# A five-stage network on one core: ScalarE and VectorE held to the order of emission, which is made with durations read from a trace

## The chip, the core and the metric

The kernel runs on one core of one Trainium2 chip. The core has a matrix engine (TensorE, PE in the profile; its weight loads are PEld), a vector engine (VectorE, DVE), a scalar engine (ScalarE, ACT), GpSimd (POOL), and SyncE (SP), which issues most of the DMAs. The metric is the device time of one execution in microseconds (us), the median of the runs.

## The reference

All data are fp32, one sequence of 1024 tokens (1040 with 16 meta tokens in the last two layers), 1024 features. Two blocks run one behind the other:

```python
def first_block(x, ...):
    f1 = swiglu(rms_norm(x, ffn1_pre_g), w_gate, w_up, w_down)      # D_FF 2816
    x = x + 0.5 * rms_norm(f1, ffn1_post_g)
    m = token_mixer(rms_norm(x, mix_pre_g), w_in, ...)              # 8 forget-gate + 4 differential heads
    x = x + rms_norm(m, mix_post_g)
    f2 = swiglu(rms_norm(x, ffn2_pre_g), ...)
    return x + 0.5 * rms_norm(f2, ffn2_post_g)

def second_block(x, meta, ...):
    h = jnp.concatenate([meta_b, x], axis=1)
    h = rglru_ssd_layer(h, ...)        # "even": conv, gated linear scan, chunked state-space scan
    h = stick_breaking_layer(h, ...)   # "odd": 16 heads of 64
    return rmsnorm(h, final_norm)[:, N_META:]

def stick_breaking_block(q_blk, k_ctx, v_ctx, q0):
    z = q_blk @ k_ctx.T * SB_HEAD_DIM ** -0.5
    log_keep = jnp.where(before, log_sigmoid(-z), 0.0)
    csum = jnp.cumsum(log_keep, axis=-1)
    weights = jnp.where(before, jnp.exp(log_sigmoid(z) + csum[..., -1:] - csum), 0.0)
    return weights @ v_ctx
```

## The kernel before

**Stages.** By the trace the first feed-forward stage runs to some 685 us, the mixer (attention of 8 + 4 heads) to some 1305, the second feed-forward stage to some 1980, the even stage to some 2740 and the odd stage (attention with 16 heads) to the end. Activations lie feature by token in SBUF as a pair `Ah`, `Al`: a value rounded to fp32r and what is left over. Each matrix product is three matmuls (`mm3`, L336 to L338: hi x hi, lo x hi, hi x lo). So every operand of TensorE comes from two instructions, one behind the other: ScalarE copies the hi half, VectorE subtracts it for the lo half. Weights (`wh`, `wl`), the transposed probabilities of attention (`th`, `tl`, written from the PSUM tile `ptr`), values (`v`, from `pv`) and activations all go through that pair.

**Attention.** `psc` are scores, ScalarE turns them into `kt` and `pt`, TensorE transposes `pt` into `ptr` (L1607), ScalarE and VectorE make `th` and `tl` of it, and TensorE multiplies them with the values into `po` (L1587). In the odd stage VectorE runs a running product over `kt` (`tensor_tensor_scan`, L2275) and a product into `pt` (L2279) for each piece of scores, ahead of the transposes. `pv` is the projection of the values of one token tile, through two PSUM buffers that VectorE frees when it has written `v`.

**Even stage.** `pe` are the projections, `xb` their copy; VectorE runs four-tap convolutions over it (`xc`, `cv`; 128x1040), products with gates (`sz`, L2601, which frees the `pe` buffer; `t`, L2609), the linear scan (`t`, L3015), and the state-space work of a chunk (`S`, `ea`, `xd`, `dec`, `et`, `ab`, `cbm`). `psx`, `psb`, `pso`, `psy`, `pst` are PSUM tiles of the latter.

**Two orders.** Work is written as generator threads. `Sched` (L109) steps the thread that can start earliest by a model of durations, with priorities; each thread yields ("A", us), ("V", us), ("P", us) ahead of an instruction of ScalarE, VectorE or TensorE, and the model's functions `act(n)`, `dve(n)` and `pool_tt(n)` give the us for n elements of a row. That sets the order in which instructions are emitted. When the program is complete, the framework's own list scheduler sets the order of each engine's queue from the dependencies, with durations of its own; in this kernel it may move instructions of every engine past each other. In the queues of before, 1141 of VectorE's 5036 instructions and 560 of ScalarE's 3228 (table loads not counted) stand behind one with a later number of emission; on TensorE it is 467 of 19667. An engine runs its queue in order. A table of ScalarE's functions is loaded where the queue needs another one (58 loads); `act_set`, `act_need` and `after_pin` tie some functions to a load.

Of the kernel before, what the change touches and what calls it, by code (L numbers as in the profile page):

```python
# [18 lines left out]
P = 128  # L19
# [3 lines left out]
L = M + S  # L23
# [73 lines left out]
def act(n):  # L97
    return 0.07 + 0.92e-3 * n


def dve(n, speed=1):
    return 0.08 + 1.045e-3 * n / speed


def pool_tt(n):
    return 0.2 + 2.1e-3 * n

# [93 lines left out]
class Ctx:  # L201
    def __init__(self, ctx, tc):
# [9 lines left out]
        self.ahead = None  # L212
        self.dr = ctx.enter_context(tc.tile_pool(name="dr", bufs=1, space=DRAM))
        self.ident = self.const.tile([P, P], F32, name="ident")
        make_identity(nc, self.ident)
# [5 lines left out]
        self.last = None  # L221
        for nm in ("activation", "copy"):
            def f(*a, _o=getattr(nc.scalar, nm), **k):
                self.last = _o(*a, **k)  # L224
                return self.last
            setattr(nc.scalar, nm, f)
        self.onesm = self.const.tile([P, P], F32, name="onesm")
        nc.vector.memset(self.onesm, 1.0)

    def new_A(self):  # L230
        return (self.ap.tile([P, KD, L], F32R, tag="Ah", name="Ah"),
                self.ap.tile([P, KD, L], F32R, tag="Al", name="Al"))

    def after_pin(self, ins):
# [6 lines left out]
    def act_set(self, name):  # L241

        ins = self.after_pin(self.nc.scalar.preload_act_table_set(name))
        if self.last is not None and self.last is not self.pin:
            self.tc.add_manual_dep(ins.ins, self.last.ins.name, mybir.DependencyInfo(
                mybir.DependencyClass.NoSync, mybir.DependencyReason.DATA), reason="table set")
        self.pin = ins

# [334 lines left out]
class Rows:  # L583
# [15 lines left out]
    def put(self, t, y, junk):  # L599
# [3 lines left out]
        if g not in self.ss:  # L603
            self.ss[g] = c.small.tile([P, len(ms)], F32, tag=f"ss{len(ms)}", name="ss", bufs=5)
        if self.dram is not None:
            r0 = self.row0 + t * P
            c.nc.scalar.dma_start(self.dram[r0:r0 + P, :], y)
        tt = yield ("A", act(1024))
        c.nc.scalar.activation(junk(), y, AF.Square, accum_out=self.ss[g][:, t - g:t - g + 1])
        self.stored[t].set(tt + 3.0)  # L610
# [1163 lines left out]
def mixer_stage(c, A, rows0, prm, w_in, forget_b, lams, subln, rope, w_out, gpost, res, rows):  # L1774
# [3 lines left out]
    with ExitStack() as ctx:  # L1778
# [18 lines left out]
        def gate_evac(lf, tok, ps):  # L1797
# [17 lines left out]
            if tok is HALVES[1]:  # L1815
                cum = pm.tile([8, S], F32, tag="bc", name="cum", bufs=2)
                yield ("V", dve(1024))
                nc.vector.tensor_tensor_scan(cum, c.one[:8].to_broadcast([8, S]), lf, 0.0, op0=ALU.mult, op1=ALU.add)
# [137 lines left out]
        def softmax(segs, m, pt, cb, ev, r):  # L1956
# [3 lines left out]
            for s, ps in enumerate(segs):  # L1960
                yield ("V", dve(m))
                if cb is not None:
# [7 lines left out]
            for s, ps in enumerate(segs):  # L1970
                t = yield ("A", act(m))
                nc.scalar.activation(pt[:, s * m:s * m + m], ps[:, :m], AF.Exp, bias=mx[:, 0:1], scale=-1.0,
                                     accum_out=sm[:, s:s + 1])
                T.r_ps["sc"].release(t)
            yield ("V", 0.2 * ns)
            if ns == 2:
# [213 lines left out]
def odd_stage(c, A, rows0, prm, w_in, w_out, res, final, out):  # L2190
# [3 lines left out]
    with ExitStack() as ctx:  # L2194
# [68 lines left out]
        def weights(ps, w, kt, k0, m, before, scanned, done):  # L2263
# [8 lines left out]

            t = yield ("V", dve(m))
            rev = kt[:, k0:k0 + m][:, ::-1]
# [224 lines left out]
def even_stage(c, A, rows0, prm, w_in, lru_wa, lru_wx, dt_bias, a_log, ssd_d, w_out, meta, res, rows, later):  # L2499
# [168 lines left out]
    def dt_rest():  # L2668
# [21 lines left out]
        nc.vector.tensor_scalar(l, dt, na, None, op0=ALU.mult)  # L2690
        yield ("V", dve(L))
        nc.vector.tensor_tensor_scan(ac, cut, l, 0.0, op0=ALU.mult, op1=ALU.add)
# [287 lines left out]
    def lru_rest(b, h, r, ig, t_, v):  # L2980
# [31 lines left out]
        for j in range(2):  # L3012
            u = 2 * b + j
            t = yield ("V", dve(LH, 0.5))
            nc.vector.tensor_tensor_scan(t_[:, j], r[:, j], v[:, j], 0.0 if h == 0 else carry[:, u:u + 1], op0=ALU.mult,  # L3015
# [293 lines left out]
```

## Time and profile before

| | us |
|---|---|
| median of 3 runs | 3579.32 |
| lowest, highest | 3578.43, 3579.59 |
| the profiled execution: own time | 3577.13 |
| its span, first to last instruction | 3575.4 |
| TensorE busy in it | 3430.7 |
| VectorE busy | 2749.9 |
| ScalarE busy | 1700.6 |
| GpSimd busy | 326.1 |

The profiled execution is 2.2 us below the median. Times in the rows below are us from the start of the span. A wait is listed by the engine that waited, the tile it wrote, and the instruction whose end released it.

### The profile page before, as it was taken

How to read it: one execution, taken by the hardware profiler on the slowest of the kernel's cores; microseconds unless marked ns; L12 is line 12 of the kernel's file. 1: busy time of each engine (PE TensorE's matmuls, PEld its weight loads, DVE VectorE, ACT ScalarE, POOL GpSimd, SP SyncE). 2: the span in 40 equal slices, each digit the busy share in tenths (PEclk: the TensorE clock that was granted, in tenths of full speed). 3: DMA queues.
4: the chain of work that ended last, by engine and by line, in shares of the span. 5: the costliest groups of instructions: out<-in, count | busy, mean ns of one | idle time of the engine just before them, and what ended most of it. 6: DMA issues, size and time to landing. Idle time of an engine off the chain costs nothing.

```text
span 3575.4 us, 51885 instructions
## 1 busy us (share of the span) xinstructions
PE 3430.7 (96%) x19675; PEld 2925.6 (82%) x19675; DVE 2749.9 (77%) x5050; ACT 1700.6 (48%) x3451; POOL 326.1 (9%) x355
## 2 busy tenths in 40 slices
PE   8999999899999999999999899998999999999998
PEld 6788888678888877888888899988878888888877
DVE  8876699988888769666799779578633688878784
ACT  5323245556666643232345447447422465656561
POOL 0111144000000001111351000000000000000000
PEclk9999999999999999999999999999999999999999
DMA  5542372311211551323552334244473110111133
GB/s 183 178 132 89 113 284 83 128 58 44 73 41 36 179 168 60 123 89 109 195 197 72 108 64 86 61 87 90 139 244 95 57 36 28 33 31 31 33 134 107
DMA packets 305842, 366.07 MB, mean 102 GB/s; under 512 B 18644, under 2 KB 221568, under 8 KB 305592
## 3 DMA queue, kind: packets, MB, share of 16 engines
q1 hardware_dynamic: 299800, 341.71, 30.7%
q10 hardware_dynamic: 5792, 21.04, 1.6%
q8 instruction: 155, 2.54, 0.3%
q14 instruction: 95, 0.78, 0.1%
HBM read 267.58 MB, written 95.13 MB: 101 GB/s over the span
## 4 chain that ended last, share of the span: by engine, by line
PE 73%; DVE 17%; ACT 4%; issue 3%; DMA 2%; SPq 0%; POOL 0%; DVEq 0%; ACTq 0%; POOLq 0%
PE pst L337 7%; PE pst L336 7%; PE pst L338 7%; PE po L1587 3%; PE pe L336 3%; PE pe L338 3%; PE pe L337 3%; DVE kt L2275 3%; PE pdn L337 2%; PE pdn L338 2%; PE pdn L336 2%; PE ptr L1607 2%; PE pwo L3100 2%; PE pwo L3101 2%; PE pwo L3102 2%
## 5 line engine op out<-in xcount | busy, mean ns | idle before, releaser
L336 PE MATMUL pe<-Ah,wh 128*128 128x260 f32 (+1 forms) x1184 | 340.6, 288 | 21.9 <-DVE sz L2601 8.2
L338 PE MATMUL pe<-Ah,wl 128*128 128x260 f32 (+1 forms) x1184 | 337.1, 285 | 0.0
L337 PE MATMUL pe<-Al,wh 128*128 128x260 f32 (+1 forms) x1184 | 336.4, 285 | 0.0
L224 ACT CAST wh<-w 128x512 fp32r<-128x512 f32 x280 | 162.1, 619 | 252.7 <-PE pst L337 160.2
L942 DVE TENSOR_TENSOR sg<-sg,pst 128x512 f32<-128x512 f32 x280 | 187.1, 684 | 104.8 <-PE pst L338 104.4
L1006 POOL TENSOR_TENSOR h<-h 128x512 f32<-128x512 f32 x88 | 136.2, 1547 | 1332.9 <-DVE h L988 1327.7
L337 PE MATMUL pst<-Al,wh 128*128 128x512 f32 x640 | 253.7, 396 | 0.0
L336 PE MATMUL pst<-Ah,wh 128*128 128x512 f32 x640 | 252.2, 394 | 0.0
L338 PE MATMUL pst<-Ah,wl 128*128 128x512 f32 x640 | 252.1, 394 | 0.0
L473 DVE TENSOR_TENSOR wl<-w,wh 128x512 fp32r<-128x512 f32 x280 | 212.0, 784 | 50.4 <-ACT wh L224 49.0
L336 PEld LDWEIGHTS pe<-Ah,wh 128*128 128x128 f32 (+1 forms) x1184 | 223.4, 189 | 26.2 <-DVE sz L2601 8.5
L337 PE MATMUL pdn<-dl,dh 128*128 128x512 f32 x592 | 230.8, 390 | 1.9 <-DVE dl L1099 1.9
L224 ACT CAST th<-ptr 128x512 fp32r<-128x512 f32 (+2 forms) x344 | 171.6, 515 | 125.4 <-PE ptr L1607 78.7
L338 PE MATMUL pdn<-dh,dl 128*128 128x512 f32 x592 | 230.3, 389 | 0.0
L1552 DVE TENSOR_TENSOR tl<-ptr,th 128x512 fp32r<-128x512 f32 (+2 forms) x344 | 197.5, 592 | 41.8 <-ACT th L224 38.4
L336 PE MATMUL pdn<-dh 128*128 128x512 f32 x592 | 229.1, 389 | 0.0
L337 PEld LDWEIGHTS pe<-Al,wh 128*128 128x128 f32 (+1 forms) x1184 | 223.0, 189 | 1.0
L338 PEld LDWEIGHTS pe<-Ah,wl 128*128 128x128 f32 (+1 forms) x1184 | 222.8, 188 | 0.8
L2275 DVE TENSOR_TENSOR_SCAN kt<-kt,onec 128x392 f32<-128x392 f32 (+5 forms) x224 | 204.2, 916 | 16.8 <-ACT kt L224 14.9
L224 ACT CAST wh<-wr 128x1024 fp32r<-128x1024 f32 (+2 forms) x116 | 119.0, 1026 | 182.7 <-PE pwo L3101 80.3
L336 PE MATMUL pst<-T,wh 128*128 128x512 f32 x480 | 187.3, 393 | 8.7 <-ACT T L224 8.7
L337 PE MATMUL pst<-T,wh 128*128 128x512 f32 x480 | 188.1, 392 | 0.4 <-DVE T L835 0.4
(550 smaller groups left out, 10023.6 us busy)
## 6 DMA issues: line engine op xcount, KB each, us to landing
hD<-h SPq DMA_DIRECT2D x22, 1792.0 KB, 8.1
w<-in_ffn_w_gate_dram SPq DMA_DIRECT2D x20, 1024.0 KB, 5.4
w<-in_ffn_w_up_dram SPq DMA_DIRECT2D x20, 1024.0 KB, 8.0
d<-hD SPq DMA_DIRECT2D x18, 1024.0 KB, 5.4
wr<-in_even_w_in_dram SPq DMA_DIRECT2D x36, 512.0 KB, 4.3
wo<-prer SPq DMA_DIRECT2D x32, 512.0 KB, 3.6
wr<-in_odd_w_in_dram SPq DMA_DIRECT2D x32, 512.0 KB, 4.3
wr<-in_w_in_dram SPq DMA_DIRECT2D x24, 512.0 KB, 3.9
```

The lines of the kernel that those rows point to most:

```text
L224: self.last = _o(*a, **k)
L336: nc.tensor.matmul(ps, wh, xh, start=start, stop=False)
L337: nc.tensor.matmul(ps, wh, xl, start=False, stop=False)
L338: nc.tensor.matmul(ps, wl, xh, start=False, stop=stop)
L473: (nc.gpsimd if eng == "G" else nc.vector).tensor_sub(lo, raw, hi.bitcast(F32))
L942: nc.vector.tensor_add(dst, src, ps)
L1006: nc.gpsimd.tensor_sub(q[:, o], q[:, a], q[:, b_])
L1552: nc.vector.tensor_sub(tl[:rows, :n], ptr[:rows, :n], th[:rows, :n].bitcast(F32))
L1587: nc.tensor.matmul(po[:, 256 - n:256], vs, (th, tl)[w][:rows, o:o + n], start=(x == 0 and y == 0 and 0 in which), stop=(x == last and y == ...
L1607: nc.tensor.transpose(ptr[:rows, o:o + P], pts[i][:, col:col + rows], c.ident)
L2275: nc.vector.tensor_tensor_scan(rev, rev, c.one.to_broadcast([P, m]), kt[:, k0 + m:k0 + m + 1], op0=ALU.mult, op1=ALU.mult)
L3100: nc.tensor.matmul(ps[n], oh, wh[:, sl], start=(first and k == 0), stop=False)
```

## The change

- The functions of the model get other numbers: `act`, `dve` and `pool_tt`, a new `scan(n)` for the four `tensor_tensor_scan` places, 0.14 us more on a mask add with a reduction, 0.19 us more on an exponential that also sums.
- Every instruction of ScalarE and VectorE that goes through the wrapped methods is recorded, and gets a dependency without a semaphore on the one recorded before it on the same engine. The list scheduler can't pass them by each other any more. TensorE, SyncE and GpSimd stay free.
- In `Rows.put` the DMA that stores the rows, issued from ScalarE's queue, stands behind the Square activation and not ahead of it.

```diff
 def act(n):
-    return 0.07 + 0.92e-3 * n
+    return 0.16 + 0.87e-3 * n
 
 
 def dve(n, speed=1):
-    return 0.08 + 1.045e-3 * n / speed
+
+    return (0.15 if speed == 1 else 0.21) + 1.05e-3 * n / speed
+
+
+def scan(n):
+    return 0.22 + 2.08e-3 * n
+
+
+ACCUM = 0.19
 
 
 def pool_tt(n):
-    return 0.2 + 2.1e-3 * n
+    return 0.2 + 2.6e-3 * n
...
-        for nm in ("activation", "copy"):
-            def f(*a, _o=getattr(nc.scalar, nm), **k):
-                self.last = _o(*a, **k)
-                return self.last
-            setattr(nc.scalar, nm, f)
+        self.tail = {}
+        self.strict = True
+
+        def record(e, ins):
+            if e == "A":
+                self.last = ins
+            if e in self.tail:
+                self.behind(ins, self.tail[e])
+            if self.strict:
+                self.tail[e] = ins
+            return ins
+
+        self.record = record
+        for e, eng, names in (("A", nc.scalar, ("activation", "copy")), ("V", nc.vector, (
...
+                def f(*a, _o=getattr(eng, nm), _e=e, **k):
+                    was, self.inner = self.inner, True
+                    ins = _o(*a, **k)
+                    self.inner = was
+                    return ins if was else record(_e, ins)
+                setattr(eng, nm, f)
...
+    def behind(self, ins, first):
+
+        self.tc.add_manual_dep(ins.ins, first.ins.name, mybir.DependencyInfo(
+            mybir.DependencyClass.NoSync, mybir.DependencyReason.DATA), reason="order of emission")
...
-        self.pin = ins
+        self.pin = self.record("A", ins)
...
+        tt = yield ("A", act(1024))
+        c.nc.scalar.activation(junk(), y, AF.Square, accum_out=self.ss[g][:, t - g:t - g + 1])
         if self.dram is not None:
             r0 = self.row0 + t * P
-            c.nc.scalar.dma_start(self.dram[r0:r0 + P, :], y)
-        tt = yield ("A", act(1024))
-        c.nc.scalar.activation(junk(), y, AF.Square, accum_out=self.ss[g][:, t - g:t - g + 1])
+            c.behind(c.nc.scalar.dma_start(self.dram[r0:r0 + P, :], y), c.last)
...
-            t = yield ("V", dve(m))
+            t = yield ("V", scan(m))
             rev = kt[:, k0:k0 + m][:, ::-1]
             nc.vector.tensor_tensor_scan(rev, rev, c.one.to_broadcast([P, m]), kt[:, k0 + m:k0 + m + 1],
```

The number of instructions is the same, but for ScalarE's table loads: 54 in place of 58. The queues differ nearly everywhere: 359 of VectorE's 5036 instructions keep their place in it. The lists below call a scan SCALAR_TENSOR_TENSOR too. In the queues of the change 96 of VectorE's instructions and 4 of ScalarE's stand behind one with a later number of emission, and 546 of TensorE's. All recorded instructions carry L251, the line of the wrapper.

The first of two places is VectorE's queue in the odd stage, where two heads' scans and the values of one token tile meet. The rows of before (`v4`, `v5`: the values of two heads; `tl`: lo halves of transposed probabilities):

```order
L1552 TENSOR_TENSOR tl_30252<-ptr_30250,th_30251 128x512
L1505 TENSOR_TENSOR v4_29862<-pv_30201,v4_29862 128x128
L1552 TENSOR_TENSOR tl_30271<-ptr_30269,th_30270 128x384
L1505 TENSOR_TENSOR v5_29864<-pv_30201,v5_29864 128x128
L2275 SCALAR_TENSOR_TENSOR kt_30285<-kt_30285,onec_76 128x392
L2279 TENSOR_TENSOR pt_30284<-pt_30284,kt_30285 128x392
L2275 SCALAR_TENSOR_TENSOR kt_30285<-kt_30285,onec_76 128x392
L2279 TENSOR_TENSOR pt_30284<-pt_30284,kt_30285 128x392
L1632 TENSOR_TENSOR oo_30205<-po_30234,ot_30332 64x256
```

The same place with the change, VectorE again:

```order
L251 SCALAR_TENSOR_TENSOR kt_30395<-kt_30395,onec_76 128x352
L251 TENSOR_TENSOR pt_30394<-pt_30394,kt_30395 128x352
L251 SCALAR_TENSOR_TENSOR kt_30395<-kt_30395,onec_76 128x344
L251 TENSOR_TENSOR pt_30394<-pt_30394,kt_30395 128x344
L251 SCALAR_TENSOR_TENSOR kt_30395<-kt_30395,onec_76 128x344
L251 TENSOR_TENSOR pt_30394<-pt_30394,kt_30395 128x344
L251 SCALAR_TENSOR_TENSOR kt_30419<-kt_30419,onec_76 128x456
L251 TENSOR_TENSOR pt_30416<-pt_30416,kt_30419 128x456
L251 SCALAR_TENSOR_TENSOR kt_30419<-kt_30419,onec_76 128x456
L251 TENSOR_TENSOR pt_30416<-pt_30416,kt_30419 128x456
L251 TENSOR_TENSOR v5_29860<-pv_30223,v5_29860 128x128
L251 TENSOR_TENSOR v4_29858<-pv_30273,v4_29858 128x128
```

Before, a pair `v4`, `v5` of one `pv` stands between the `tl` and ahead of the scans of `kt`. Now the `v5` of `pv_30223` and both of `pv_30273` come behind five scans and their products.

The second place is VectorE's queue in the even stage, in the first pass over a chunk of the state-space work. Before, around the update of the state `S`:

```order
L473 TENSOR_TENSOR wl<-wr,wh 128x1024
L2609 TENSOR_TENSOR t<-t,sz 128x260
L2770 TENSOR_SCALAR ab<-ab,dT 128x128 x4
L2826 TENSOR_TENSOR S_18696<-S_18696,et 128x512
L2835 TENSOR_TENSOR ea<-ea,pso 128x512
L3002 TENSOR_TENSOR v<-v,t 128x1040
L2601 TENSOR_TENSOR sz<-sz,pe 128x260
L2828 TENSOR_TENSOR S_18696<-S_18696,pst 128x512
L2838 TENSOR_TENSOR ea<-ea,psy 128x512
L2749 TENSOR_TENSOR cbm<-psb,mask_tri 128x128
```

The same place with the change, from the last of `xc` to the gate product `sz` that frees the projection's buffer:

```order
L251 SCALAR_TENSOR_TENSOR xc_18371<-xc_18371,dcol,ea 128x128
L251 SCALAR_TENSOR_TENSOR xc_18490<-xc_18490,dcol,ea 128x128
L251 TENSOR_TENSOR cbm<-psb,mask_tri 128x128
L251 SCALAR_TENSOR_TENSOR t<-r,carry,v 128x520
L251 TENSOR_TENSOR xd<-psx,dT 128x512
L251 TENSOR_TENSOR dec<-ab,dT 128x8
L251 COPY et<-ab 128x8
L251 TENSOR_SCALAR ab<-ab,dT 128x128 x8
L251 CAST lh<-cv_19271 128x520
L251 TENSOR_TENSOR ll<-cv_19271,lh 128x520
L251 TENSOR_TENSOR t<-t,sz 128x260
L251 TENSOR_TENSOR sz<-sz,pe 128x260
```

Before, `sz` comes two places behind the `ea` that reads `pso`. Now it stands behind both updates of `S`, both of `ea`, the four `xc`, `cbm`, a scan, `xd` and the eight `ab` of the next chunk.

## Rows read from the trace of the kernel before

**Rows 1.** The page: span; busy us of each engine (share, instructions)

```profile
span 3575.4 us, 51885 instructions
...
PE 3430.7 (96%) x19675; PEld 2925.6 (82%) x19675; DVE 2749.9 (77%) x5050; ACT 1700.6 (48%) x3451; POOL 326.1 (9%) x355
```

**Rows 2.** The page: the chain that ended last, share by engine

```profile
PE 73%; DVE 17%; ACT 4%; issue 3%; DMA 2%; SPq 0%; POOL 0%; DVEq 0%; ACTq 0%; POOLq 0%
```

**Rows 3.** Waits of TensorE, whole span: us, times, longest us

```profile
PE po L1587 <- DVE tl L1552: 22.2, 31, 2.8
PE po L1587 <- ACT th L224: 10.6, 13, 1.5
...
PE pst L336 <- ACT T L224: 8.7, 4, 4.0
PE pe L336 <- DVE sz L2601: 8.2, 1, 8.2
PE psx L2747 <- ACT xc L224: 7.2, 1, 7.2
...
PE pe L336 <- DVE Al L565: 6.2, 1, 6.2
PE ptf L577 <- DVE xr L626: 5.4, 4, 2.1
...
PE pd L336 <- DVE Al L565: 4.8, 1, 4.8
...
PE pe L336 <- ACT xb L224: 3.5, 1, 3.5
```

**Rows 4.** Three stretches: length, busy us of engines, granted clock, DMA share, GB/s

```profile
95.00:115.00 20.00, 13.84 (x45) 9.94 (x45) 20.00 (x34) 6.66 (x10) 0.00 (x0) 0.74 0.57 209
200.00:300.00 100.00, 100.00 (x437) 81.70 (x436) 70.64 (x105) 30.57 (x55) 18.14 (x12) 1.00 0.35 119
2430.00:2450.00 20.00, 11.76 (x85) 10.73 (x84) 19.64 (x36) 12.58 (x19) 0.00 (x0) 0.74 0.43 68
```

**Rows 5.** The core's span and mean granted clock of TensorE

```profile
core 0: 3575.4 us, clock 0.987
```

**Rows 6.** VectorE's timeline, even stage: start us, length us, then the operation

```profile
2187.23 1.66 DVE L2770 TENSOR_SCALAR ab<-ab,dT 128x128 f32<-128x128 f32 x8
...
2435.06 1.24 DVE L3010 TENSOR_TENSOR v<-v,ig 128x1040 f32<-128x1040 f32 x1
2436.22 0.69 DVE L2826 TENSOR_TENSOR S<-S,et 128x512 f32<-128x512 f32 x1
2436.82 1.30 DVE L3015 TENSOR_TENSOR_SCAN t<-r,carry,v 128x520 f32<-128x520 f32 x1
2438.03 0.67 DVE L2828 TENSOR_TENSOR S<-S,pst 128x512 f32<-128x512 f32 x1
...
2441.21 1.12 DVE L2845 SCALAR_TENSOR_TENSOR xc<-xc,dcol,ea 128x128 f32<-128x128 f32 x4
2442.24 0.69 DVE L2759 TENSOR_TENSOR xd<-psx,dT 128x512 f32<-128x512 f32 x1
2442.84 0.70 DVE L2942 TENSOR_TENSOR ll<-cv,lh 128x520 fp32r<-128x520 f32 x1
2443.45 0.76 DVE L2601 TENSOR_TENSOR sz<-sz,pe 128x260 f32<-128x260 f32 x2
```

**Rows 7.** VectorE by line and shape, odd stage: busy us, mean ns

```profile
L1552 DVE TENSOR_TENSOR tl<-ptr,th 128x512 fp32r<-128x512 f32 x96 | 64.6, 684 | 3.6 <-ACT th L224 2.5
...
L2275 DVE TENSOR_TENSOR_SCAN kt<-kt,onec 128x456 f32<-128x456 f32 x32 | 37.1, 1161 | 1.8 <-ACT kt L224 1.6
...
L2275 DVE TENSOR_TENSOR_SCAN kt<-kt,onec 128x344 f32<-128x344 f32 x32 | 29.7, 929 | 0.2
...
L2279 DVE TENSOR_TENSOR pt<-pt,kt 128x456 f32<-128x456 f32 x32 | 20.1, 628 | 1.2
L1505 DVE TENSOR_TENSOR v<-pv,v 128x128 fp32r<-128x128 f32 x64 | 18.2, 284 | 16.8 <-ACT v L224 16.5
```

More of the change, by code (lines that the diff above doesn't have):

```diff
@@ L213, in __init__ @@
         self.dr = ctx.enter_context(tc.tile_pool(name="dr", bufs=1, space=DRAM))
+        self.inner = False
         self.ident = self.const.tile([P, P], F32, name="ident")
@@ L221, in __init__ @@
         self.last = None
-        for nm in ("activation", "copy"):
-            def f(*a, _o=getattr(nc.scalar, nm), **k):
-                self.last = _o(*a, **k)
-                return self.last
-            setattr(nc.scalar, nm, f)
+        self.tail = {}
[10 more added lines that the diff above has]
+        for e, eng, names in (("A", nc.scalar, ("activation", "copy")), ("V", nc.vector, (
+                "memset", "reciprocal", "reduce_sum", "scalar_tensor_tensor", "stream_shuffle", "tensor_add",
+                "tensor_copy", "tensor_mul", "tensor_reduce", "tensor_scalar", "tensor_sub", "tensor_tensor",
+                "tensor_tensor_reduce", "tensor_tensor_scan"))):
+            for nm in names:
+                def f(*a, _o=getattr(eng, nm), _e=e, **k):
[4 more added lines that the diff above has]
+                setattr(eng, nm, f)
         self.onesm = self.const.tile([P, P], F32, name="onesm")
@@ L1816, in gate_evac @@
                 cum = pm.tile([8, S], F32, tag="bc", name="cum", bufs=2)
-                yield ("V", dve(1024))
+                yield ("V", scan(1024))
                 nc.vector.tensor_tensor_scan(cum, c.one[:8].to_broadcast([8, S]), lf, 0.0, op0=ALU.mult, op1=ALU.add)
@@ L1960, in softmax @@
             for s, ps in enumerate(segs):
-                yield ("V", dve(m))
+                yield ("V", dve(m) + (0.14 if cb is not None else 0))
                 if cb is not None:
@@ L1970, in softmax @@
             for s, ps in enumerate(segs):
-                t = yield ("A", act(m))
+                t = yield ("A", act(m) + ACCUM)
                 nc.scalar.activation(pt[:, s * m:s * m + m], ps[:, :m], AF.Exp, bias=mx[:, 0:1], scale=-1.0,
@@ L1974, in softmax @@
                 T.r_ps["sc"].release(t)
-            yield ("V", 0.2 * ns)
+            yield ("V", 0.16 * ns)
             if ns == 2:
@@ L2690, in dt_rest @@
         nc.vector.tensor_scalar(l, dt, na, None, op0=ALU.mult)
-        yield ("V", dve(L))
+        yield ("V", scan(L))
         nc.vector.tensor_tensor_scan(ac, cut, l, 0.0, op0=ALU.mult, op1=ALU.add)
@@ L3013, in lru_rest @@
             u = 2 * b + j
-            t = yield ("V", dve(LH, 0.5))
+            t = yield ("V", scan(LH))
             nc.vector.tensor_tensor_scan(t_[:, j], r[:, j], v[:, j], 0.0 if h == 0 else carry[:, u:u + 1], op0=ALU.mult,
```

## Prediction

> **What bounds the kernel now.** I read the page first. TensorE is busy for 3430.7 us of a span of 3575.4, VectorE for 77%, ScalarE for 48% [rows 1]; at full clock TensorE starts 437 matmuls of 512 columns in 100 us, one each 0.229 us [rows 4]. So the kernel is bound by TensorE, and what a change of order can move is the time in which TensorE stands or runs at half clock. The chain of work that ended last says who makes it stand: VectorE holds 17% of it and ScalarE 4% [rows 2]. The list of waits then names the places [rows 3]. Two kinds are in it. Many short ones: products `po` that wait for `th` or `tl`, 32.8 us in 44 waits. And a few long ones, each in one place: `sz` 8.2, `xc` 7.2, `Al` 6.2 and 4.8, `xb` 3.5, four on `T` with 8.7, four on `xr` with 5.4. Last the clock: the mean is 0.987 [rows 5], that is 0.013 x 3575 = 46 us of TensorE's time lost at 1.2 in place of 2.4 GHz. In stretches around a long wait the mean is 0.74, in an undisturbed one 1.00 [rows 4].
>
> **What the change does, part by part.** It adds no work. The new numbers of the model move nothing by themselves but the order of emission; the model is nearer to the rows than before (a scan of 456 elements takes 1161 ns [rows 7]; the old function says 557, the new one 1168). Four table loads fewer are ScalarE's, which has half its span free: nothing. The store behind the Square is one activation later, for rows that are read again a stage later: nothing, and if a reader did wait, that one activation. What counts is the chain of dependencies. Before, the list scheduler could put a short `tl`, `v` or `sz` ahead of long work that nobody waits for yet. Now the queue is the emission order, and a late entry holds all behind it. So I took the queues of both kernels and asked, for each wait of TensorE on ScalarE or VectorE, how much TensorE work lies between the last matmul that the operand depends on and the matmul that needs it, and how much queue has to be run in the meantime.
>
> (a) *Short waits of attention, mixer and odd stage.* By the queues 35 products `po` of before have less than 1 us of TensorE work as cover, and 118 with the change; 69 of these are the direct way transposes, `th`, product. The 32.8 us of before [rows 3] over 35 such places are 0.94 us each. 83 more would be 78 us at that price; none if the operands come early anyhow. Neighbours share a wait, since TensorE's standing lets the queues catch up, so I take half: **+39**, ends 0 and +78.
>
> (b) *Values behind scans, odd stage* (the first place in the order). The PSUM buffer of `pv` comes free when `v5` is written, and `v5` now ends a run that begins at two `tl` of 512: 17 VectorE instructions. By recorded means: two `tl` 1.37, three scans of 456 3.48, four products `pt` of that size 2.51, three scans and three products of about 344 2.8 and 1.5, a short `tl` 0.55, `v` 0.28: 12.5 us. Rows show that one instruction starts before the one ahead has ended by its record: an `S` of 0.69 us is followed after 0.60, a scan of 1.30 after 1.21 [rows 6]. With 0.085 off for each the run takes 11.1. TensorE has 51 matmuls in that time, mostly pieces of 128 to 456 columns, 6.0 us at the rate of rows 4. So the next `pv` waits 5.1 us, in three rounds of the odd stage the same; a shorter run of the same make (eight scans and products, then `v`) holds a `po` by some 2.5 each time. 3 x 7.6 = **+23**, ends 0 and +35.
>
> The Trainium skill (VectorE: DVE Perf Modes, The DRAIN you can't avoid) says that the next VectorE operation doesn't start until the pipe of the one before is empty. Rows 6 show starts 0.09 us ahead of the recorded end. By the page's rule the run would be 12.5 us, the wait 6.5, and this term +27; the sum goes by the rows.
>
> (c) *Even stage* (the second place). From `S` to `sz` the queue of the change holds two `S` and two `ea` of 0.60 each, `xc` 1.03, a scan 1.21, `xd` 0.60, eight `ab` 1.66, `ll` 0.61, `t` and `sz` 0.38 each, `cbm` some 0.2: 8.5 us [rows 6], small ones left out. Ahead of it stand `v` 1.16 and a scan 1.21, for which ScalarE has a long way to go. TensorE has 24 matmuls of 260 columns and the transposes in the meantime, 3.8 us. So `sz` is 4.7 late, or 7.1 if `v` is: +7. The third pass keeps its 8.2 of today, as +1. At the end of the state-space work two such runs and the products with `sz` follow each other; I estimate +14, from twice the 7.1, with ends 0 and +20. Two more `sz` behind eight steps of convolution or a weight split: +4 each. Against that the waits on `xc` and `xb` go, 7.2 and 3.5 [rows 3], since their copies are no longer passed by others. Sum 7 + 1 + 14 + 8 - 10.7 = **+19**, ends -11 and +40.
>
> (d) *Start, projections, seams of stages.* The queues show the same late entries for `T`, for `xr` at the start (two weight splits and a second chain of small instructions stand ahead of it) and for weights at the seam of mixer and second feed-forward stage. No row prices them; the nearest are the 8.7 and 5.4 of today, and I take that once more: **+14**, ends 0 and +28.
>
> (e) *Ends of the feed-forward stages.* `Al` comes earlier in the queue. Of 6.2 and 4.8 [rows 3] I take 7 away: **-7**, ends -11 and 0.
>
> (f) *Clock.* Today 46 us are lost beside the long waits of rows 3, which sum to 44 us: about one for one. (b) to (d) add 56 us, most of it in waits over 2 us. At half clock TensorE's work covers more of the next wait, so I take little more than a third: **+20**, ends 0 and +46.
>
> Sum: 39 + 23 + 19 + 14 - 7 + 20 = +108 on the execution's own 3577.13, 3685; the median of the runs stands 2.2 higher, so **3687**, +3.0%.
>
> **Rivals.** *The order of emission is the better one (faster).* The place is the long waits: `sz`, `xc`, `T`, `Al`, `xb` together 38.6 us [rows 3]. They stand where the scheduler let work of a later chunk pass. If the emission order, with true lengths of scans, puts each operand just ahead of its matmul, they go, with some of the clock that they cost: 3579 - 39 - 5 = 3535. It decides from the point at which the cover of the products `po` stays longer than the way through ScalarE and VectorE, 0.6 to 0.7 us each [rows 7]; then (a) and (b) are nil. For it: the model fits the rows, and ScalarE and VectorE have free time. Against it: the queues, where tight products grow from 35 to 118.
>
> *VectorE's queue becomes the bound of the attention stages (much slower).* At 77% busy, with each wait of VectorE passed on to all behind it, delays needn't be caught up between two rounds. Then (a) comes at its full 78, (b) 35, (c) 40, (d) 28 and the clock at 30: 3579 + 211 - 7 = 3783. For it: over the odd stage scans, products and `tl` come back to back. Against it: TensorE's standing gives VectorE time, and today its share is 77%, not 90.
>
> *TensorE's free order makes up for it (no change).* The list scheduler still orders TensorE's queue, with the chains known to it: 546 instructions of it stand behind later ones, 467 before. If it put other matmuls into each hole, the time would be 3579 within 7. Against it: the covers above are counted in its finished queue. That the change doesn't do what it says is out for the same reason: 96 of VectorE's and 4 of ScalarE's instructions are left out of the emission order.
>
> **How the numbers follow.** The forecast has 0.72, much slower 0.13, faster 0.10, no change 0.05. A measurement of this kernel can tell about 0.2% from no change, 7 us. The forecast's own spread is wide, since (a) and (f) are halves of their ends: all terms low give 3557, all high 3806, halfway to the low ends 3622, halfway to the high ones 3746. To leave out no more than 2 in 10, with faster and no change outside below (0.15), the range goes from 3595 to 3785. Faster by over 0.2% 0.10, within 0.2% 0.05, slower 0.85.
>
> **What would show it.** The list of TensorE's waits: `po` on `th` and `tl` beyond 50 us in over 80 waits, a wait of `pv` on `v` of about 5 us three times in the odd stage, `pe` on `sz` more than twice its 8.2, no wait of `psx` on `xc`. The granted clock at 0.98 or lower. VectorE's busy time unchanged within 1%, ScalarE's about 5 us down. The forecast is wrong if the waits on `tl` and `th` stay near 33 us: then the covers don't tell the waits. (b) is wrong if `pv` doesn't wait, (c) if `sz` stands in one place as now.

## The result, and the profile after

The changed kernel takes 3797.35 us (median; 3795.36 to 3802.54), the kernel before 3578.88: 1.061 times as long, interval 1.060 to 1.0626. Slower was forecast, with 3687 and a range up to 3785; the loss is 218 us where 108 were forecast, just outside the range. Of the executions below one, of E6, took 6162 us at a mean granted clock of 0.77; it is left out of that kernel's time.

The page of the changed kernel: span, busy time of each engine, and the chain that ended last, by engine, to be read beside [rows 1] and [rows 2].

```profile
span 3797.3 us, 51813 instructions
...
PE 3515.3 (93%) x19675; PEld 2978.9 (78%) x19675; DVE 2859.8 (75%) x5050; ACT 1699.2 (45%) x3447; POOL 336.2 (9%) x355
...
PE 73%; DVE 17%; ACT 5%; issue 2%; DMA 2%; SPq 0%; DVEq 0%; ACTq 0%; POOL 0%; POOLq 0%
```

TensorE is busy for 84.6 us more with the same 19675 matmuls, and it stands for 137 us more (3797.3 - 3515.3 = 282.0, before 144.7). The chain's shares hardly differ from before: the loss is spread over the whole kernel, not one new piece. Most of the longer busy time goes with the mean granted clock; it was 0.987 [rows 5]:

```profile
core 0: 3797.3 us, clock 0.965
```

In the clock's records of the two traces the granted clock is half of the full one in 42 pieces that sum to 269 us, before in 17 that sum to 92. Half of that is 134 and 46 us. TensorE works in 189 and 66 us of these pieces and stands in what is left of them, so the work that it lost lies between 95 and 134 us, before between 33 and 46.

What TensorE waited for (us in total, times, longest us; its order by size), to be read beside [rows 3]. All lines of ScalarE and VectorE are L251, the wrapper's.

```profile
PE psy L2839 <- DVE ab L251: 29.1, 5, 13.4
PE pe L369 <- DVE sz L251: 22.5, 4, 7.7
PE po L1620 <- DVE tl L251: 21.4, 25, 2.8
PE pdn L370 <- DVE dl L251: 18.2, 11, 5.0
PE pv L1558 <- DVE v L251: 16.5, 7, 5.0
PE po L1620 <- DVE v L251: 14.0, 5, 3.3
PE ptr L1640 <- DVE pt L251: 12.6, 10, 3.0
PE psc L1573 <- ACT pt L251: 10.5, 22, 1.2
PE ptf L610 <- DVE xr L251: 9.6, 1, 9.6
...
PE pe L369 <- ACT sz L251: 6.9, 1, 6.9
...
PE po L1620 <- ACT th L251: 5.7, 11, 1.3
...
PE pd L369 <- DVE Al L251: 1.7, 1, 1.7
...
PE psx L2780 <- ACT xc L251: 0.7, 1, 0.7
PE pe L369 <- DVE Al L251: 0.7, 1, 0.7
```

Three lines of before, for comparison; no wait of `pv` or `po` on `v` was over 0.4 us there:

```profile
PE psy L2806 <- DVE ab L2781: 3.2, 2, 2.5
...
PE pdn L337 <- DVE dl L1099: 1.9, 4, 0.6
...
PE ptr L1607 <- DVE pt L1994: 1.0, 1, 1.0
```

Three things stand here. New waits on VectorE where before there was little: `ab`, `dl` (the lo half of an operand of the down projection `pdn`), `v` twice, `pt`. The wait on `sz`, once 8.2 long, is there four times. And the products `po` wait for `tl` and `th` 27.1 us in 36 places, less than the 32.8 in 44 of before [rows 3]: in the odd stage they fell from 29.6 to 14.5 us, in the mixer they rose from 3.2 to 12.5. The waits on `xc` and on `Al` are all but gone.

By stages (first feed-forward, mixer, second feed-forward, even, odd; each ends with the start of its last `pdn` or `pwo` matmul; columns as in [rows 4]), before and after:

```profile
0.00:675.50 675.50, 654.69 (x2862) 535.05 (x2863) 552.64 (x830) 268.82 (x466) 150.54 (x89) 0.99 0.44 148
675.50:1303.50 628.00, 601.84 (x3570) 504.08 (x3570) 515.69 (x1334) 369.33 (x908) 3.11 (x6) 0.99 0.26 82
1303.50:1969.60 666.10, 656.06 (x2869) 535.37 (x2868) 538.05 (x798) 255.84 (x451) 146.86 (x80) 0.99 0.37 127
1969.60:2776.10 806.50, 767.42 (x5514) 696.50 (x5513) 522.48 (x947) 372.65 (x605) 8.68 (x40) 0.98 0.41 107
2776.10:3565.80 789.70, 750.21 (x4865) 654.63 (x4864) 616.74 (x1130) 432.81 (x1022) 16.92 (x140) 0.99 0.17 55
```

```profile
0.00:698.70 698.70, 661.41 (x2862) 536.45 (x2863) 589.23 (x835) 271.09 (x467) 153.06 (x89) 0.99 0.42 143
698.70:1380.50 681.80, 624.81 (x3570) 516.43 (x3569) 530.45 (x1325) 369.12 (x903) 3.54 (x6) 0.96 0.23 74
1380.50:2074.50 694.00, 664.93 (x2869) 539.37 (x2868) 579.75 (x808) 260.08 (x455) 150.60 (x80) 0.97 0.36 123
2074.50:2931.60 857.10, 784.20 (x5514) 709.77 (x5512) 532.49 (x939) 366.93 (x597) 11.20 (x40) 0.95 0.39 100
2931.60:3787.70 856.10, 779.57 (x4866) 676.88 (x4864) 623.64 (x1132) 430.80 (x1024) 17.78 (x140) 0.96 0.16 51
```

Length less TensorE's busy time is its standing: 20.8, 26.2, 10.0, 39.1, 39.5 us before; 37.3, 57.0, 29.1, 72.9, 76.5 after. So every stage stands longer: by 16, 31, 19, 34 and 37 us.

### The profile page after: what moved, and what is told of

It is laid out like the page before. It is cut to its first block, busy times and chain, and to the rows that moved or that the text cites. A ratio compares the mean times of both kernels' runs of the same rounds, so it can differ in the third digit from the quotient of the medians.

```text
span 3797.3 us, 51813 instructions
## 1 busy us (share of the span) xinstructions
PE 3515.3 (93%) x19675; PEld 2978.9 (78%) x19675; DVE 2859.8 (75%) x5050; ACT 1699.2 (45%) x3447; POOL 336.2 (9%) x355
## 3 DMA queue, kind: packets, MB, share of 16 engines
q1 hardware_dynamic: 299800, 341.71, 29.1%
## 4 chain that ended last, share of the span: by engine, by line
PE 73%; DVE 17%; ACT 5%; issue 2%; DMA 2%; SPq 0%; DVEq 0%; ACTq 0%; POOL 0%; POOLq 0%
PE pst L370 6%; PE pst L369 6%; PE pst L371 6%; PE pe L369 3%; PE pe L371 3%; PE pe L370 3%; PE po L1620 3%; DVE kt L251 2%; PE pdn L370 2%; PE pdn L371 2%; PE pdn L369 2%; DVE dl L251 2%; PE ptr L1640 2%; DVE acc L251 2%; PE pwo L1769 2%
## 5 line engine op out<-in xcount | busy, mean ns | idle before, releaser
L369 PE MATMUL pe<-Ah,wh 128*128 128x260 f32 (+1 forms) x1184 | 344.4, 291 | 30.8 <-DVE sz L251 22.5
L251 DVE TENSOR_TENSOR sg<-sg,pst 128x512 f32<-128x512 f32 x280 | 186.0, 684 | 135.3 <-PE pst L371 133.8
L251 ACT CAST wh<-w 128x512 fp32r<-128x512 f32 x280 | 160.7, 617 | 213.6 <-PE pst L370 76.8
L370 PE MATMUL pdn<-dl,dh 128*128 128x512 f32 x592 | 234.0, 395 | 18.2 <-DVE dl L251 18.2
L251 DVE TENSOR_TENSOR tl<-ptr,th 128x512 fp32r<-128x512 f32 (+2 forms) x344 | 197.9, 592 | 69.4 <-ACT th L251 65.9
L251 DVE TENSOR_TENSOR wl<-w,wh 128x512 fp32r<-128x512 f32 x280 | 238.2, 889 | 13.2 <-ACT wh L251 12.4
L251 ACT CAST th<-ptr 128x512 fp32r<-128x512 f32 (+2 forms) x344 | 169.5, 515 | 154.8 <-PE ptr L1640 133.9
L251 DVE TENSOR_TENSOR_SCAN kt<-kt,onec 128x392 f32<-128x392 f32 (+5 forms) x224 | 205.3, 916 | 12.1 <-ACT kt L251 10.0
L1640 PE MATMUL ptr<-ident,pt 128*128 128x128 f32 x1136 | 183.3, 281 | 14.8 <-DVE pt L251 12.6
```

The costliest lines, as they stand in the source:

```text
L251: ins = _o(*a, **k)
L369: nc.tensor.matmul(ps, wh, xh, start=start, stop=False)
L370: nc.tensor.matmul(ps, wh, xl, start=False, stop=False)
L1640: nc.tensor.transpose(ptr[:rows, o:o + P], pts[i][:, col:col + rows], c.ident)
```

## The two places of the order, in the trace

The first place, odd stage. VectorE's timeline of the changed kernel (start us, length us, operation), and TensorE's line with what ended its wait:

```profile
3211.08 0.68 DVE L251 TENSOR_TENSOR tl<-ptr,th 128x512 fp32r<-128x512 f32 x1
3211.68 1.16 DVE L251 TENSOR_TENSOR_SCAN kt<-kt,onec 128x456 f32<-128x456 f32 x1
...
3219.99 1.16 DVE L251 TENSOR_TENSOR_SCAN kt<-kt,onec 128x456 f32<-128x456 f32 x1
3221.25 0.63 DVE L251 TENSOR_TENSOR pt<-pt,kt 128x456 f32<-128x456 f32 x1
3221.80 0.48 DVE L251 TENSOR_TENSOR v<-pv,v 128x128 fp32r<-128x128 f32 x2
```

```profile
3222.14 0.58 PE L1558 MATMUL pv<-wh,Ah 128*128 128x256 f32 x1 [5.00 <-DVE v L251]
```

VectorE is in the run of scans and products when TensorE asks for the `pv` buffer; the first of the two `v` starts at 3221.80, TensorE at 3222.14 after 5.00 us. The prediction had 5.1. The wait comes three times at 5.0 (it ends at 3222, 3407 and 3592 us), and a `po` waits for `v` four times for 3.1 to 3.3.

The second place, even stage, first pass. TensorE, then VectorE:

```profile
2278.30 0.59 PE L369 MATMUL pe<-Ah,wh 128*128 128x260 f32 x1 [6.06 <-DVE sz L251]
```

```profile
2266.14 1.24 DVE L251 TENSOR_TENSOR v<-v,ig 128x1040 f32<-128x1040 f32 x1 [0.35 <-ACT v L251]
...
2268.71 0.67 DVE L251 TENSOR_TENSOR S<-S,et 128x512 f32<-128x512 f32 x1
...
2274.84 1.66 DVE L251 TENSOR_SCALAR ab<-ab,dT 128x128 f32<-128x128 f32 x8
...
2277.83 0.42 DVE L251 TENSOR_TENSOR sz<-sz,pe 128x260 f32<-128x260 f32 x1
```

`sz`, from 2277.83 to 2278.25, ends a run that begins with `v` at 2266.14: 12.1 us, and TensorE stood for 6.06. The prediction had 10.9 for the run and 7 for the wait.

## Experiments

The table shows all of them at once; each one's reason follows. "Standing" is the span less TensorE's busy time, "clock" half of the time at half clock (TensorE's standing in that time counted too), "rest" the span less both. The stages' lengths are made as above.

| kernel | median us | ratio, interval | standing | clock | rest | ffn 1 | mixer | ffn 2 | even | odd |
|---|---|---|---|---|---|---|---|---|---|---|
| before | 3579 | | 145 | 46 | 3385 | 675.5 | 627.9 | 666.1 | 806.5 | 789.8 |
| the change | 3797 | 1.060 to 1.063 | 282 | 134 | 3381 | 698.7 | 681.7 | 694.1 | 857.1 | 856.1 |
| E1 durations alone, no chain | 3624 | 1.011 to 1.014 | 165 | 57 | 3398 | 672.9 | 634.5 | 667.5 | 830.2 | 805.6 |
| E2 chains alone | 3708 | 1.035 to 1.038 | 230 | 101 | 3376 | 695.0 | 668.4 | 690.3 | 833.1 | 809.8 |
| E3 chain on ScalarE only | 3712 | 1.036 to 1.039 | 225 | 86 | 3399 | 687.8 | 665.4 | 683.3 | 831.2 | 832.0 |
| E4 chain on VectorE only | 3806 | 1.062 to 1.065 | 284 | 136 | 3382 | 695.6 | 684.8 | 693.3 | 860.5 | 858.1 |
| E5 scans at the old price | 3746 | 1.046 to 1.049 | 248 | 119 | 3379 | 698.7 | 682.1 | 694.8 | 850.5 | 809.7 |
| E6 only scans at the new price | 3737 | 1.043 to 1.047 | 243 | 103 | 3389 | 694.8 | 669.4 | 690.6 | 833.6 | 837.4 |
| E7 evictions first | 3756 | 1.048 to 1.051 | 261 | 121 | 3372 | 695.5 | 678.3 | 695.1 | 858.4 | 816.8 |
| E8 as E1, scans at the old price | 3605 | 1.006 to 1.010 | 158 | 50 | 3394 | 672.7 | 637.8 | 666.8 | 825.0 | 789.4 |
| E9 chain over 4 places | 3713 | 1.036 to 1.039 | 214 | 113 | 3384 | 685.2 | 662.1 | 681.5 | 845.2 | 826.6 |
| E10 chain over 16 places | 3649 | 1.018 to 1.021 | 190 | 79 | 3383 | 675.3 | 644.7 | 671.7 | 832.7 | 818.9 |
| E11 feed-forward stages free | 3755 | 1.048 to 1.051 | 246 | 120 | 3384 | 673.7 | 681.4 | 672.4 | 856.0 | 857.7 |
| E12 store alone | 3581 | 1.000 to 1.002 | 143 | 52 | 3384 | 677.6 | 626.4 | 666.8 | 809.6 | 788.9 |

### E1 and E2: the two halves of the change apart

E1 takes the chains out of the change:

```diff
-        self.strict = True
+        self.strict = False
```

> The change without its chains: the new durations, the new place of the store, but no dependency between neighbours on ScalarE and VectorE, so the list scheduler may reorder both queues as before. My theory (the chains cost the time): within 0.5% of the kernel before, 3562 to 3597 us, the mean clock back at 0.98 or more, pv waiting for v under 1 us in all. The rival (the new durations make a worse order of emission, which would be slow in any hands): over 3650 us.

Measured: 3624 us. Neither theory: the chains make most of the loss, but the durations alone cost 45 us, with both queues free. The waits of TensorE:

```profile
PE pe L369 <- DVE sz L251: 11.5, 3, 5.3
...
PE psx L2780 <- ACT xc L251: 6.7, 1, 6.7
```

Two long waits of before are still there: `xc` with 6.7 (7.2 before), and `sz`, now 11.5 in three places (8.2 in one). `pv` doesn't wait for `v`.

E2 puts `record`, `behind` and the wrappers into the kernel before, and nothing else:

```diff
...
+            if e in self.tail:
+                self.behind(ins, self.tail[e])
+            if self.strict:
+                self.tail[e] = ins
...
```

> The chains without the new durations: the kernel before with ScalarE and VectorE tied to its old order of emission; the store stays where it was. My theory (the chains cost the time, the durations matter little): 3740 to 3860 us, that is 4 to 8% slower than before. The rival (the chains are harmless and the new durations do the harm): under 3650 us. If the new durations help the chained order, this run is slower than the change's 3797 us; if they hurt it, faster.

Measured: 3708 us, below the 3740 that I expected at the least: 129 us for the chains with the old durations. So 45 and 129 make 174, and 44 more come from the two together. The waits:

```profile
PE po L1612 <- DVE tl L243: 31.8, 39, 2.6
...
PE pdn L362 <- DVE dl L243: 17.6, 10, 5.1
PE pe L361 <- DVE sz L243: 15.1, 3, 10.1
```

The long wait on `sz` (10.1 in one place, 15.1 in three) and those on `dl` come with the chains alone. No `pv` of the odd stage waits for `v` longer than 0.5 us here: that place needs the new durations as well.

### E3 and E4: which engine's chain

```diff
-            if self.strict:
+            if self.strict and e == "A":
```

> The change with the chain on ScalarE alone; VectorE's queue is free again. My theory: TensorE's long waits of the change are released by VectorE (v, sz, ab, dl), so most of the time comes back: 3590 to 3650 us, the waits on v, sz and ab at the size of the kernel before. The rival (a late ScalarE instruction holds VectorE up, since nearly each lo half follows a hi half): over 3700 us.

> The change with the chain on VectorE alone; ScalarE's queue is free again. My theory: nearly all of the loss stays, 3740 to 3810 us. The rival (ScalarE's chain is what counts): under 3680 us. If the two losses add up, this one's and that of the chain on ScalarE alone together make the 218 us of the change.

E4 has `"V"` in the same line. Measured: 3712 and 3806 us. The chain on VectorE alone is as bad as both, as expected; the chain on ScalarE alone, which I had at 3590 to 3650, came out as the rival said. Both kernels have the new durations, so E1 with 3624 is what they start from: ScalarE's chain costs 88 us, VectorE's 182, both together 173. The two don't add up, and VectorE's is the whole of it. ScalarE's chain works through VectorE, which has none in E3: what TensorE waits for VectorE goes from 82 us in E1 to 135, what it waits for ScalarE from 61 to 63. That fits the rival's reason, that VectorE's lo half follows ScalarE's hi half.

### E5, E6 and E8: which durations

E5 gives the four scans their old price; E8 does the same without chains; E6 gives all others theirs and keeps the scans' new one:

```diff
 def scan(n):
-    return 0.22 + 2.08e-3 * n
+    return (0.08 + 2.09e-3 * n) if n == LH else (0.08 + 1.045e-3 * n)
```

> The change with the old price of the scans alone (456 elements 0.56 us in the model, not 1.17); the other new durations, the chains and the store stay. With old durations the chains cost 130 us, with the new ones 218: 88 us belong to the durations. Theory A (the scans' price is what counts: in the model VectorE is busier by some 140 us in the odd stage, and work of low priority, such as writing the values or the gate product, is emitted behind it): 3700 to 3730 us, the waits of pv on v under 3 us. Theory B (the fixed part per instruction, 0.07 to 0.13 us more on each of 8000, does it): over 3770 us.

> The change with all durations as before but the scans' new price; chains and store stay. Theory A (the scans' price): 3770 to 3810 us, pv waits for v as in the change, some 16 us. Theory B (the fixed parts): 3700 to 3730 us. If both this one and the run with the old scan price alone lie near 3750, the two shares add up.

> The new durations without chains, but with the old price of the scans. With the new price this cost 45 us against the kernel before, 24 of them in the even and 16 in the odd stage. Theory A (the scans' price): 3575 to 3592 us. Theory B (the fixed parts of each instruction, or the store): 3610 us or more.

Measured: 3746, 3737 and 3605 us. Neither theory: chained, the old price of the scans gives back 51 us, the old price of the rest 60, where both together (E2, which has the old store too) give 89. The two overlap by 22, and the stages separate them. In the odd stage nothing is lost to the durations without the scans' price: 809.7 with the old one, as with no new duration at all (E2, 809.8), and 856.1 with the new one. The scans' price alone makes 28 of these 46 us (E6, 837.4); the other 19 come only where both meet, and so do the waits of `pv` on `v`: 2.6 us in all in E5, 3.1 in E6, 16.5 in the change. Without chains the odd stage takes 789.4 (E8) and 805.6 (E1), beside 789.8 before. In the mixer, which has one small scan, it is the rest: 669.4 (E6) and 682.1 (E5). In the even stage E6 is at 833.6, as E2 with 833.1, and E5 at 850.5: mostly the rest, too. Without chains the rest still costs 18 us there and 10 in the mixer (E8 beside before).

### E7: why a truer price puts `v` late

The scheduler takes the thread that can start first, and at equal start the one with the better priority: 0 for the transposes' copies, 1 for scans, 3 for the threads that write values and projections out of PSUM. Where the model holds VectorE for busy, several threads are ready when it comes free, and the priority decides. E7 lifts those writers:

```diff
-            self.sch.spawn(self.evac_v(us, x, T, ps, diff), 3, t)
+            self.sch.spawn(self.evac_v(us, x, T, ps, diff), 0, t)
...
-            sch.spawn(evac(ps, tok, i, bank), 3, t)
+            sch.spawn(evac(ps, tok, i, bank), 0, t)
```

> The change with one more edit: the threads that write the values out of pv and the even stage's projections out of pe get priority 0 in the model in place of 3, so that at equal start they are emitted ahead of scans, products and state-space work. If priorities under a VectorE that the model takes as busy are why v and sz stand late, the waits on v (16.5 and 14.0 us) and on sz (22.5) fall under 10 in all, and with the clock 55 to 75 us come back: 3720 to 3745 us. The rival (something else in the queue holds TensorE at the same places, the waits only change their names): over 3780 us.

Measured: 3756 us, between the two. In the odd stage the theory holds: 856.1 to 816.8 us, and the waits of `pv` and of `po` on `v`, 16.5 and 14.0 in the change, are gone but for 0.2 us; part of them came back under another name, `ptr` on `pt`, from 10.6 to 22.4 us in that stage. In the even stage the rival holds: 857.1 and 858.4 us. The waits there have another name, `wl`:

```profile
PE psy L2839 <- DVE ab L251: 29.0, 6, 11.7
PE pe L371 <- DVE wl L251: 26.6, 3, 9.4
```

26.6 us on weight halves in three places, where the change had 22.5 on `sz` in four: with `sz` ahead, the next weight's lo half stands behind, and `psy` waits for `ab` as before the edit. So in the even stage it isn't the place of one instruction that counts.

### E9 and E10: how far an instruction must be free to move

```diff
-            if e in self.tail:
-                self.behind(ins, self.tail[e])
-            if self.strict:
-                self.tail[e] = ins
+            row = self.tail.setdefault(e, [])
+            if len(row) >= 4:
+                self.behind(ins, row[-4])
+            row.append(ins)
```

> The change with its chains loosened: each instruction is tied to the one emitted four places earlier on its engine, not to its neighbour, so the list scheduler may pass a few places. Without chains the new durations give 3624 us, with tight ones 3797. Theory N (near passes are what the chains forbid: one tl or v ahead of a scan or two): half or more of the 173 us come back, under 3710 us. Theory F (the late operands stand behind runs of ten to twenty instructions, so only long passes help): over 3750 us.

> The same with sixteen places. Theory N: 3620 to 3650 us, as without chains. Theory F: still 3660 us or more, since a seam of stages and the end of the state-space work need passes of more than sixteen; the waits of pv on v, behind a run of 17, are gone in either case.

E10 has 16 in both places. Measured: 3713 and 3649 us. Of the 173 us between tight chains and none, 4 places give back 85 and 16 places 148. So about half is near passes, at the edge of theory N (under 3710 us), 63 us are passes of 4 to 16 places, and 25 longer ones. With 4 places `pv` still waits for `v` three times, 8.9 in all, and `pdn` for `dl`:

```profile
PE pdn L370 <- DVE dl L251: 10.7, 8, 3.7
...
PE pv L1558 <- DVE v L251: 8.9, 3, 3.0
```

With 16 places, about the length of the run ahead of `v`, that wait isn't listed any more, and `dl` is down to 2.3. `ab` and `sz` stay longer than in E1 (9.5 and 11.5):

```profile
PE psy L2839 <- DVE ab L251: 20.1, 7, 7.3
...
PE pe L369 <- DVE sz L251: 16.0, 2, 8.0
...
PE pdn L370 <- DVE dl L251: 2.3, 6, 0.6
```

But the even stage as a whole is only 2.5 us above E1 by then; what is left is in the mixer (10 us) and in the odd stage (13 us), and it wasn't followed to single places.

### E11: does a stage's loss stay in the stage

```diff
 def ffn_stage(...):
+    c.strict = False
...
         sch.run()
+        c.strict = True
```

> The change without chains in the two feed-forward stages; the other three keep them. By the stages' own lengths (698.7 and 694.1 us with the change, 672.9 and 667.5 without any chain) and if a stage's loss stays in the stage: 52 us back, 3735 to 3755 us, the waits of pdn on dl from 18 to under 4. The rival (the queues run over from stage to stage, so that the loss comes back in the next one): over 3775 us.

Measured: 3755 us, 43 back. The two stages come to 673.7 and 672.4 us (before the edit 698.7 and 694.1), the other three keep their length within 2 us. So the loss of these two stages stays in them, and a stage can be judged from the part of a queue that belongs to it. Of the waits:

```profile
PE pdn L370 <- DVE dl L251: 1.9, 4, 0.8
```

`dl` falls from 18.2 to 1.9. In the changed kernel the last `dl` of the stage stands behind the end of four rows of output (`acc`, eight operations of 1.2 us), and TensorE stood 5.0 and 4.9 us for it at the ends of the two stages.

### E12: the store

```diff
...
+        tt = yield ("A", act(1024))
+        c.nc.scalar.activation(junk(), y, AF.Square, accum_out=self.ss[g][:, t - g:t - g + 1])
         if self.dram is not None:
             r0 = self.row0 + t * P
-            c.nc.scalar.dma_start(self.dram[r0:r0 + P, :], y)
-        tt = yield ("A", act(1024))
-        c.nc.scalar.activation(junk(), y, AF.Square, accum_out=self.ss[g][:, t - g:t - g + 1])
+            c.behind(c.nc.scalar.dma_start(self.dram[r0:r0 + P, :], y), c.last)
```

> The kernel before with one part of the change, the store of the rows behind the Square activation on ScalarE's queue; old durations, no chains. My prediction took it at nothing: 3572 to 3586 us. The rival (the rows are read back late, or the list scheduler's order turns over at another place of emission): over 3590 us, which would be a part of the 28 us that the new durations without the scans' price cost without chains.

Measured: 3581 us, 1.0007 times the kernel before, interval 0.9998 to 1.0017. Nothing, as the prediction took it; under chains it wasn't tried by itself.

## Why the prediction was wrong, step by step

The side, the bound and most of the places were right; the sum was half of what came. By its steps:

**(f), the clock, was the largest miss: +20 forecast, +88 measured.** I had argued that TensorE's work at half clock covers more of the next wait, and so had taken little more than a third of what the rows of before gave, about one for one. No run tests that argument; what the table shows is that the cost came. In all fourteen kernels TensorE's busy time is the lost clock plus a rest of 3372 to 3399 us, and the lost clock follows the standing: a straight line through the fourteen gives 0.64 us for each us of standing more (E9 lies 21 us off it). Had I known that, the forecast's own 88 us of waits would have brought 56 for the clock, not 20, and the sum would have been +144. The 88 measured is the upper count. Only TensorE's work at half clock counted, it is 62 (95 less 33), 0.46 us for each us of standing; the busy time grew by 84.6, and what made the 23 us between isn't shown.

**(a), the short waits of attention, was wrong in its mechanism.** The waits of `po` on `tl` and `th` fell from 32.8 to 27.1 us though products with less than 1 us of cover went from 35 to 118; the prediction had named exactly this as its refutation. The price was loose from the start: it spread the time of 44 waits over 35 places. In the mixer the waits did grow, by 9 us; in the odd stage they fell by 15. There a product with little cover doesn't wait if TensorE has just stood for something else, and the runs bear this out. Where the odd stage's waits of `pv` and `po` on `v` and of `ptr` on `pt` come to 22 us or more (the change, E4, E7, E9, E11; 41 in the change), `po` waits 8 to 16 us for `tl` and `th`; where they stay under 6 us (before, E1, E2, E5, E8, E10, E12), 27 to 37; E3 and E6 lie between. The standing of both attention stages grew by 68 us together, where (a) and (b) had 62. So the size was about right for another reason: luck. Counting tight places by itself didn't tell the waits.

**(b), values behind scans, was right in place and size:** 5.0 us three times for 5.1, and 3.1 to 3.3 four times for 2.5 three times. But it needs both halves of the change. The order shows the place, not its cause: with durations alone (E1) no `pv` of the odd stage waits for `v`, with chains alone (E2) for 0.5 us at most.

**(c), the even stage, was right in its places and too small:** `sz` 6.1 for 7 in the first pass, four waits in all as forecast; `xc` and `xb` nearly gone, as forecast. The mis-sized term is the end of the state-space work, +14 forecast: there `psy` waits for `ab` 13.4 and 7.5 us, and a `pe` for ScalarE's `sz` 6.9, 28 us in one stretch of 40, where the same waits of before came to 5. The longest of them shows what the sum of run lengths left out. ScalarE, VectorE twice, and TensorE:

```profile
2637.09 1.04 ACT L251 CAST wh<-wor 128x1024 fp32r<-128x1024 f32 x1 [2.59 <-DMA wor<-in_even_w_out_dram]
```

```profile
2638.17 1.23 DVE L251 TENSOR_TENSOR wl<-wor,wh 128x1024 fp32r<-128x1024 f32 x1 [4.16 <-ACT wh L251]
2639.31 1.22 DVE L251 TENSOR_TENSOR ab<-ab,cbm 128x1024 f32<-128x1024 f32 x1
```

```profile
2640.58 1.98 PE L2839 MATMUL psy<-ab,xd 128*64 128x128 f32 x16 [13.43 <-DVE ab L251]
```

`ab` stands in the queue behind the lo half of an output weight whose data are still on their way. So VectorE itself stands for 4.16 of the 13.43 us, with `ab` next in its queue and ScalarE's part in `ab` done at 2634.5. The prediction added up lengths of instructions and had no term for a queue that stands. The stage's standing grew by 34 us where +19 was the sum.

**(d) and (e) came about as forecast, +14 and -7, but left out the largest new wait of the feed-forward stages.** The waits that (d) named grew by 14 us: `xr` from 5.4 to 9.6, `T` from 9.1 to 14.0, and the weights at the seam (`w0h`, `w0l`) from none to 4.7. `Al` did come earlier (0.7 and 1.7 us in place of 6.2 and 4.8), as (e) had it. Yet the two feed-forward stages stand 35 us longer. What I didn't look for, and so put at nothing, is what came to stand late in its place: `dl`, 18.2 us in 11 waits, before 1.9 in 4. In the mixer two waits at the projections were missed in the same way, `pg` on `rx` (0.5 to 7.0 us) and `pv` on `wl` (none to 5.9).

**The durations** were taken at nothing but their effect through the chains. They cost 45 us alone (E1). That the model fits the rows better didn't make its order better.

Sum: the standing was forecast at +88 and is +137; the clock at +20 and is +88; the rest is 4 lower. That is the 222 us between the two spans. Beside the terms one of the signs failed: VectorE's busy time was to stay within 1% and rose by 4%.

Of the rivals, the much slower one (3783) came nearest, but not by its mechanism: it had (a) at its full 78, and VectorE isn't the bound of the attention stages, being busy for 78% of the mixer and 73% of the odd stage. Of the rule on the page VectorE: DVE Perf Modes of the Trainium skill (The DRAIN you can't avoid), weighed in (b), the changed kernel shows the same as the rows did: in the first timeline above a `tl` of 0.68 us is followed after 0.60, and the wait was 5.0, not 6.5. The same section says that an operation which isn't held starts earlier; no run here shows which are held.

No order tried here beats the kernel before.

**What stays open.** Which of the other constants (the fixed part for ScalarE, for VectorE, the 0.19 or the 0.14) costs the 60 us of E6 wasn't taken apart. Nor was the mixer's loss under the chains (40 us) followed to single places; its waits are spread over `psc`, `po`, `pv` and `ptr`.

## What to carry to other kernels

An order of emission with strict queues makes all that is behind a late operand late; before tying queues to it, compare the finished queues and add up, for each run of instructions that a matmul now waits behind, its length less TensorE's work in that time. Long runs ahead of one operand (here 17 and 27 instructions) gave the wait to within 1 us where the queue kept working; look, too, for an instruction in the run that has to wait for a transfer or for another engine, since then the queue stands (here 4.2 us). Counting operands with little cover didn't tell the waits. Add to each us of new standing its share of lost clock as the traces at hand show it (here 0.46 to 0.64), and if a model of durations is made truer, look again at the priorities that were tuned with the old one: work of low priority that used to find a gap finds none when the model holds the engine for busy.

## What the runs showed of the hardware

The fall of the clock came on top of the standing in every order of the same work: while standing went from 143 to 284 us, half of the time at half clock went from 46 to 136 us, and TensorE's busy time from 3431 to 3519. Around the 5.00 us wait that ends at 3222.14 the clock's records have 6.8 us at 1.2 GHz. They begin 2.6 us into the wait, TensorE works in 4.4 of them, and so the wait of 5.0 us cost 2.2 more. With the two others of the kind it was 1.8 and 1.6.

VectorE's own work got longer without a change of operation: 2749.9 us before, 2859.8 after, with the same 5050 instructions, and 78 of these 110 us lie in the feed-forward stages. It goes with the chains: 2743 to 2751 us in the orders with both queues free (before, E1, E8, E12) and with 16 places (E10), 2854 to 2861 wherever VectorE is tied to its neighbour throughout. The lo halves of weights in the feed-forward stages (128x512) took 784 ns in the mean before and 889 after. The traces show which of the 280 are slow: those beside which GpSimd has an operation for over a fifth of their length, 56 before with 1172 ns in the mean and 70 after with 1500; the others take 686 and 685. `dl` is alike: 93 of 296 with 1652 ns and the others with 685 before, 107 with 1600 and the others with 682 after. No run moved GpSimd's work by itself, so the cause isn't shown by experiment, nor how much of the feed-forward stages' loss comes this way. Right ahead of the two longest waits on `dl` nothing is slow: the eight `acc` take 1.2 to 1.3 us each, as in the kernel before.
